# A feed-forward block in two stages: product buffers of the first, and where the operands of the second are formed

## The chip, the core and the metric

The kernel runs as one program on one core of a Trainium2 chip. The core's engines work side by side, each through its own queue of instructions in order: TensorE (PE, with PEld for its weight loads), VectorE (DVE), ScalarE (ACT), GpSimd (POOL), and SyncE (SP), which issues most of the DMAs. The metric is the device time of one execution in microseconds, as the median of several runs. Before the change it is 3231.77 us (3 runs, 3229.75 to 3237.66).

## What is computed

A two-layer encoder over 1024 tokens of width 1024. Each layer has four mixers, an output projection with a layer norm, the feed-forward block, and a gated embedding with its layer norm. The feed-forward block, with 2816 inner features, is what the change touches:

```python
gate = dwconv_centred(h @ ffn_w_gate[i], ffn_conv_w[i], ffn_conv_b[i])
f = (jax.nn.silu(gate) * (h @ ffn_w_up[i])) @ ffn_w_down[i]
h = layer_norm(ALPHA * h + f, ln2_g[i], ln2_b[i])
```

All is float32. The kernel keeps that precision by splitting each matmul operand into a high and a low part and summing three products (`p3`).

## The kernel before

The inner features are 22 tiles of 128 (`NF`). `gate_up` (L1355) goes over them one by one. Up and gate of a tile are the two rows of a 2 x 2 block product (halves of the width by halves of the tokens), and Winograd's scheme makes it in seven products of half size instead of eight. A product (`product`, L1378) is four blocks of the contraction by three terms, so 12 matmuls of 128 x 512 into one PSUM bank, from the pool `ps1` with four banks. The pool `ps2` with two tiles of two banks is not used by these products.

For each tile, `feature` (L1396) loads the up and the gate weights into two buffers (`load`, L1368, tile name wraw), forms the sum `s1` (tile s) and three differences, and splits five of them into high and low parts (`part`, L1373; ScalarE writes the high part, GpSimd or DVE the low one). The readings of PSUM are DVE additions: u and u4 (tile v) from products t2 and t1, both again from t3, c11 and c12 (tile u) from products 21 and 22, and the halves of g from t3 and t4. ScalarE reads product 11 into v1. `gated` (L1427) does the tile before: a convolution along the tokens (one ScalarE and two DVE steps), Silu on ScalarE, and the product with c11 on DVE and with c12 on GpSimd. Both halves, 256 KB each, are stored to DRAM (`fd`, L1434).

`down` (L1462) multiplies the features with the down weights. For the first 20 tiles (`PAIRED`) `down_paired` (L1511) uses the same scheme of seven products on pairs of tiles, four tiles (a chunk) at a time, so five chunks. `operands` (L1528) loads the four feature tiles (fr) and the four weight tiles (wr, wraw), forms the combinations (`comb`) of the features on DVE, with a spare tile (tg), and those of the weights on GpSimd, and splits each operand: features' low parts on GpSimd, weights' low parts on DVE (`part`, L1522). `products` (L1571) then runs 24 matmuls for each of the seven products (L1582): product 1 collects in PSUM over all chunks, products 5 to 7 are added to tiles E, the others to H, on DVE (ScalarE in the first chunk of E). The last chunk also runs `merge` (L1597). The last two tiles go a plain way (`CHUNKS`).

The program says which engine does what. The order within each engine's queue is written by a planner when the kernel is built: it takes the instructions by their place in the program as soon as it reckons their inputs and buffers to be ready. Of a pool's buffers one is taken again when its last reader is done.

Of the kernel before, what the change touches and what calls it, by code (L numbers as in the profile page):

```python
# [28 lines left out]
# columns of the packed per-layer parameters  # L29
# [4 lines left out]
# feature tiles of the input projection  # L34
# [8 lines left out]
def interleave(*flows):  # L43
    """Emits flows, each (generator, number of its steps), in step with one another."""
    live = [[g, 0, n] for g, n in flows]
    while live:
        f = min(live, key=lambda f: f[1] / f[2])
        try:
            next(f[0])
            f[1] += 1  # L50
        except StopIteration:
            live.remove(f)


def stagger(items):
    """Emits the stages of items so that each item is one stage behind the one before it."""
    items, live = iter(items), []
    while True:
        new = next(items, None)
        if new is not None:  # L60
            live.append(new)
        if not live:
            return
        for g in list(live):
            if next(g, live) is live:
                live.remove(g)
        yield
# [7 lines left out]
class Trunk:  # L75
# [70 lines left out]
    def to_x_after(self, x, H, t0, t1, ins, pair=False):  # L146
        """Transposes token tiles t0 to t1, once the products up to ins have freed the tiles that the
        result goes to."""
# [11 lines left out]
    def layer_norm(self, h, gb, eps=None, first=None):  # L160
        """The statistics; returns two functions that normalise h in place, one after the other."""
# [16 lines left out]
        def affine(c=512):  # L178
            """The first c columns, scaled already, on GpSimd, the others on VectorE."""
# [74 lines left out]
    def embed(self):  # L254
        """Normalises the input; the second half of the tokens only when the function that is returned runs."""
# [43 lines left out]
    def sin_of(self, fp, out, pre):  # L299
        """out = sin(pre) with the argument brought to [-pi, pi]."""  # L300
# [99 lines left out]
    def bruun(self, pool, zm, zp, C):  # L400
        """Residues of a polynomial of 1024 coefficients (8 blocks of 128 rows, C columns each)
        modulo the eight factors of x^2048 - 1 of degree 256; zm and zp are its residues modulo
        x^1024 - 1 and x^1024 + 1."""
# [36 lines left out]
    def conv_fft(self, l, n, pool, z, feature_major, out):  # L440
        """Circular convolution of z (token-major, 8 x 256) with filter n, and the skip term that the
        filter holds; the result is token-major [128, 8 * 256] or feature-major [128, 2, 8 * 128]."""
# [112 lines left out]
    def in_half(self, x, w, ps, hf):  # L555
        c0 = hf * 512
        if not isinstance(w, tuple):
            # the products of the high and the low parts of the weights, in separate rows
# [5 lines left out]
    def in_proj(self, l, x, tile_i):  # L564
        """One tile of 128 features, [128, 1024] in PSUM, in two steps."""
# [7 lines left out]
    def conv3(self, out, ps, cw):  # L573
        """Centred 3-tap convolution along the free dim with bias: cw columns w0, w1, w2, b."""
# [4 lines left out]
    def mixers(self, l, x, mu, late, st0):  # L579
# [9 lines left out]
        def scalars(su, ps):  # L589
            """Rotary key and dt, token-major."""  # L590
# [24 lines left out]
        def latent(pr, ti, k, rs, last, n):  # L615
            """A latent of attention with its gain, to DRAM; the sums of its squares go to rs."""
# [140 lines left out]
    def token_sums(self, sq):  # L757
        """Sums over features of the tiles sq [128 features, 512 tokens], as [128, 4] with tokens on partitions."""
# [5 lines left out]
    def squares(self, ss, g, hf, y, sq):  # L764
        """For the sums of squares of group g for 512 tokens, whose features are y, tokens on partitions:
        returns the function that finishes them on the tensor engine."""
# [6 lines left out]
    def ssd_scalars(self, l, mu, dtr):  # L773
# [5 lines left out]
        # softplus(x) = max(x, 0) + log1p(exp(-|x|)), the log by its series in e / (2 + e)  # L779
# [32 lines left out]
        # log(dt) - acs  # L812
# [6 lines left out]
    def ssd(self, l, ss, scal, xbc, zd, yd):  # L819
# [17 lines left out]
        def jv(a, c, g, n):  # L837
            """Columns (direction, head) of a group, broadcast over n."""
            return a[:, c, :].rearrange("p (d h) -> p d h", d=2)[:, :, 2 * g:2 * g + 2].unsqueeze(3).to_broadcast([128, 2, 2, n])

        def states(c, g):
            # token-major x and B, chunk states, forward scan
# [92 lines left out]
    def hl_products(self, out, terms):  # L935
        """Products of a [K, 2, 64] (hi and lo) with b, hi and lo: the sum of out[0:64] and out[64:128]."""
# [228 lines left out]
    def out_weights(self, l, g, pool):  # L1165
        """The rows of the output projection of a group, times the gains of its norm."""
# [12 lines left out]
    def out_proj(self, l, st, yd, ss, w, ahead):  # L1179
        nc, t = self.nc, self.t  # L1180
        hp = self.pool(st, f"hp{l}", 8, side=RIGHT)
        with ExitStack() as so:
# [17 lines left out]
            def scales(g):  # L1200
                # the residual branch is left unscaled: H holds the sum over ALPHA
# [73 lines left out]
    def blocks(self, todo, j):  # L1275
        """Transposes blocks of 128 tokens and 512 features, each (from, PSUM, (hi, lo)), to the
        128 tokens j of the operands."""
# [10 lines left out]
    def rest(self, l, st, H, hp, hmid, x):  # L1288
        nc, t = self.nc, self.t
        last = l == L - 1  # L1290
        fd = self.dram.tile([NF, 128, T], F32, name=f"f{l}")
# [63 lines left out]
    def gate_up(self, l, H, hp, x, fd):  # L1355
        """The inner features of the MLP, to fd. Up and gate are the two rows of a product of blocks
        A (features x halves of D) and B (halves of D x halves of the tokens), by Winograd's scheme
        of seven products."""
        nc, t, pp = self.nc, self.t, self.pp[l]
        add, sub = ALU.add, ALU.subtract  # L1360
        with ExitStack() as st:
# [16 lines left out]
            def product(w, b):  # L1378
                ps = self.one()
# [4 lines left out]
            def first(w1, w2, eng=None):  # L1384
                """The products of the first row of A and the first column of B."""
                v1, c11 = small(), fu.tile([128, 512], F32, name="u", tag="u")
# [9 lines left out]
            def feature(f, last, start=None):  # L1396
# [12 lines left out]
                w4 = part(a12, hp, "H")  # L1409
                u = small()  # L1410
                self.tt(u, product(w2, B["t2"]), v1, add)
                u4 = small()
                self.tt(u4, product(w1, B["t1"]), u, add)
# [8 lines left out]
                self.tt(g[:, 0:512], product(w22, B["t4"]), u, add)  # L1422
                c12 = fu.tile([128, 512], F32, name="u", tag="u")
                self.tt(c12, product(w4, B["22"]), u4, add)
                return f, g, c11, c12

            def gated(f, g, *cc):  # L1427
# [3 lines left out]
                for hf, c in enumerate(cc):  # L1431
                    cs = slice(hf * 512, (hf + 1) * 512)
                    self.tt(c, c, tg[:, cs], ALU.mult, nc.gpsimd if hf else nc.vector)
                    nc.sync.dma_start(fd[f][:, cs], c)  # L1434
# [8 lines left out]
            for j in range(4):  # L1443
# [3 lines left out]
                # T1 = B12 - B11, T3 = B22 - B12, T2 = B22 - T1, and B21 - T2 for T4  # L1447
# [14 lines left out]
    def down(self, l, fd, hmid, H, end, ed):  # L1462
        nc, t, pp = self.nc, self.t, self.pp[l]
        with ExitStack() as st:
# [30 lines left out]
            self.down_paired(l, fd, hmid, H, dp, ft)  # L1495
# [15 lines left out]
    def down_paired(self, l, fd, hmid, H, dp, ft):  # L1511
        """ALPHA times H plus the products of the first PAIRED inner features, by Winograd's scheme of seven
        products: A (halves of the tokens x two tiles of features) times B (the two tiles x halves of the outputs)."""
# [14 lines left out]
        def operands(ch):  # L1528
            """The operands of the seven products of two pairs of feature tiles, one after the other."""
            F, W = {}, {}  # L1530
            for k in (0, 2, 1, 3):
                f = 4 * ch + k
                F[k] = self.wp.tile([128, T], F32, name="fr", tag="whl", bufs=4)
                nc.sync.dma_start(F[k], fd[f])
# [8 lines left out]
            a11, a12, a21, a22 = ([F[2 * i + k][:, h] for i in range(2)] for h in (h0, h1) for k in range(2))  # L1543
            b11, b21, b12, b22 = ([W[2 * i + k][:, h] for i in range(2)] for h in (h0, h1) for k in range(2))
            s1 = ft.tile([128, T], F32, name="tg")
            s1 = [s1[:, h0], s1[:, h1]]
# [257 lines left out]
```

## Time and profile before

| | us |
|---|---|
| median of 3 runs | 3231.77 |
| lowest, highest run | 3229.75, 3237.66 |
| span of the profiled execution | 3236.6 |
| PE busy | 2976.9 (92%) |
| DVE busy | 2451.0 (76%) |
| GpSimd busy | 1821.3 (56%) |
| ScalarE busy | 1292.0 (40%) |
| gate and up, layer 0 (819 to 1250) | 431 |
| paired down, layer 0 (1250 to 1475) | 225 |

The span is the time from the first to the last instruction of one profiled execution. Matmuls overlap one another, so a busy PE is not a PE at its best rate. In the profile a line of the kernel can be that of a helper: L99 is every matmul of `mm`, L87 every two-operand operation of `tt`, L84 every ScalarE step. Tile names tell them apart. A timeline row gives the start, the time, the engine, the line, the operation, the written and the read tiles, the shape, the count of instructions merged, and in brackets the idle time ahead and what ended it.

### The profile page before, as it was taken

The numbers are of one execution on the slowest core, as the hardware profiler recorded it, in microseconds if no ns is written. First come the engines' busy times: TensorE is split into PE (matmuls) and PEld (weight loads), VectorE is DVE, ScalarE is ACT, GpSimd is POOL, SyncE is SP. The second block draws the span as 40 slices with busy tenths as digits, with TensorE's granted clock in tenths as the row PEclk, the third lists the DMA queues.
The fourth block names the chain that finished last, engine by engine and source line by source line (L and its number), as shares of the span: only waits on it lengthen the run. The fifth ranks groups of instructions, "written<-read, shape, count | busy, mean of one in ns | idle before, by whom it ended". The sixth has DMA issues, their size and how long they took to land.

```text
span 3236.6 us, 40462 instructions
## 1 busy us (share of the span) xinstructions
PE 2976.9 (92%) x14316; PEld 2429.1 (75%) x14316; DVE 2451.0 (76%) x3711; ACT 1292.0 (40%) x2278; POOL 1821.3 (56%) x1371
## 2 busy tenths in 40 slices
PE   6999989998999999999989998899989999989996
PEld 4887866877777777777868877778777777767685
DVE  7678776878765557999777786778786555689986
ACT  4332365743333334333343323667333333343341
POOL 5455533527656556886435454345177555578855
PEclk9999998999999999999999998999999999999998
DMA  5566523022222225313335755130222222343232
GB/s 178 156 200 204 192 75 130 16 83 85 85 79 78 78 79 198 123 47 115 126 100 172 225 192 165 53 121 25 97 85 79 79 78 78 114 163 107 74 135 92
DMA packets 140468, 368.98 MB, mean 114 GB/s; under 512 B 15139, under 2 KB 42023, under 8 KB 140009
## 3 DMA queue, kind: packets, MB, share of 16 engines
q1 hardware_dynamic: 126008, 315.72, 28.8%
q0 software_dynamic: 14256, 50.67, 5.2%
q8 instruction: 114, 1.87, 0.2%
q14 instruction: 90, 0.73, 0.1%
HBM read 278.77 MB, written 87.56 MB: 113 GB/s over the span
## 4 chain that ended last, share of the span: by engine, by line
PE 39%; DVE 21%; POOL 16%; issue 10%; DMA 10%; ACT 4%; SPq 0%; POOLq 0%; DVEq 0%; ACTq 0%
PE ps L99 18%; PE pp L99 13%; POOL w L87 5%; DMA wraw<-in_ffn_w_gate_dram 4%; POOL wraw L87 4%; DVE part L87 3%; POOL u L87 2%; DVE fr L87 2%; POOL H L87 2%; PE ps L942 2%; DVE H L90 2%; DVE s L87 1%; POOL part L87 1%; DVE H L87 1%; DMA wraw<-in_ffn_w_up_dram 1%
## 5 line engine op out<-in xcount | busy, mean ns | idle before, releaser
L99 PE MATMUL ps<-x,w 128*128 128x512 f32 x2112 | 508.2, 394 | 11.3 <-ACT v L84 6.1
L99 PEld LDWEIGHTS ps<-x,w 128*128 128x128 f32 x2112 | 400.1, 190 | 99.1 <-ACT v L84 7.0
L99 PE MATMUL pp<-x,wh 128*128 128x512 f32 x1344 | 427.9, 397 | 1.8 <-ACT wh L84 1.8
L99 PE MATMUL ps<-xq,w 128*128 128x512 f32 x1584 | 391.1, 397 | 29.7 <-DVE u L87 24.3
L1582 PE MATMUL ps<-part 128*128 128x512 f32 x1440 | 351.2, 399 | 33.8 <-DVE H L87 10.8
L99 PEld LDWEIGHTS ps<-xq,w 128*128 128x128 f32 x1584 | 292.9, 188 | 117.2 <-DVE u L87 50.7
L1582 PEld LDWEIGHTS ps<-part 128*128 128x128 f32 x1440 | 270.9, 191 | 110.5 <-DVE H L87 20.3
L99 PEld LDWEIGHTS pp<-x,wh 128*128 128x128 f32 x1344 | 254.9, 192 | 54.3 <-ACT wh L84 2.0
L87 POOL TENSOR_TENSOR w<-wraw,w 128x512 fp32r<-128x512 f32 x164 | 217.5, 1345 | 116.0 <-ACT w L84 116.0
L99 PE MATMUL pp<-x,wl 128*128 128x512 f32 x672 | 266.5, 397 | 3.8 <-POOL wl L87 3.8
L84 ACT ACTIVATE w<-wraw 128x512 fp32r<-128x512 f32 x264 | 151.8, 622 | 268.0 <-DMA wraw<-in_ffn_w_up_dram 218.6
L87 POOL TENSOR_TENSOR wl<-wraw,wh 128x1024 fp32r<-128x1024 f32 (+2 forms) x61 | 152.8, 2507 | 182.7 <-ACT wh L84 124.2
L87 POOL TENSOR_TENSOR part<-fr,part 128x512 fp32r<-128x512 f32 x120 | 192.4, 1628 | 47.2 <-ACT part L84 42.2
L87 DVE TENSOR_TENSOR s<-wraw 128x512 f32<-128x512 f32 x44 | 55.4, 1259 | 202.2 <-DMA wraw<-in_ffn_w_gate_dram 199.8
L99 PE MATMUL ps<-wo,yn 128*128 128x512 f32 x768 | 189.7, 405 | 5.4 <-DVE H L90 3.0
L1039 POOL TENSOR_TENSOR P<-P,smr 128x1024 f32<-128x1024 f32 x64 | 121.1, 1893 | 112.2 <-DVE smr L1038 103.3
L99 PEld LDWEIGHTS ps<-wo,yn 128*128 128x128 f32 x768 | 147.1, 195 | 39.4 <-DVE H L90 4.8
L90 DVE SCALAR_TENSOR_TENSOR g<-g,pp 128x1023 f32<-128x1023 f32 x88 | 126.6, 1439 | 57.7 <-ACT g L84 57.7
L87 POOL TENSOR_TENSOR u<-u,g 128x512 f32<-128x512 f32 x44 | 78.7, 1788 | 152.5 <-ACT g L84 152.3
L87 DVE TENSOR_TENSOR part<-wr,part 128x512 fp32r<-128x512 f32 x124 | 158.2, 1299 | 4.8 <-ACT part L84 4.8
L99 PE MATMUL ps<-wh,x 128*128 128x512 f32 x512 | 158.8, 391 | 0.0
L99 PEld LDWEIGHTS pp<-x,wl 128*128 128x128 f32 x672 | 128.5, 191 | 30.5 <-POOL wl L87 4.7
(381 smaller groups left out, 7038.7 us busy)
## 6 DMA issues: line engine op xcount, KB each, us to landing
c_fwd<-in_c_fwd_dram POOLq DMA_DIRECT2D x64, 512.0 KB, 5.1
wraw<-in_ffn_w_up_dram SPq DMA_DIRECT2D x50, 512.0 KB, 3.5
wraw<-in_ffn_w_gate_dram SPq DMA_DIRECT2D x44, 512.0 KB, 4.5
f<-u SPq DMA_DIRECT2D x88, 256.0 KB, 2.0
wraw<-in_w_in_dram SPq DMA_DIRECT2D x42, 512.0 KB, 4.1
fr<-f SPq DMA_DIRECT2D x40, 512.0 KB, 4.5
wr<-in_ffn_w_down_dram SPq DMA_DIRECT2D x36, 512.0 KB, 6.4
c_inv<-in_c_inv_dram POOLq DMA_DIRECT2D x32, 512.0 KB, 5.0
```

The lines of the kernel that those rows point to most:

```text
L84: self.nc.scalar.activation(out, in_, func, **kw)
L87: (eng or self.nc.vector).tensor_tensor(out, a, b, op=op)
L90: return self.nc.vector.scalar_tensor_tensor(out, a, s, b, op0=op0, op1=op1)
L99: ins = self.nc.tensor.matmul(out, a, b, start=i == 0, stop=i == n - 1)
L942: ins = self.nc.tensor.matmul(out[0:64] if j else out, v[:, 0, :] if j else v.rearrange("p i d -> p (i d)"), terms[i][1 + j], start=k == 0 ...
L1039: nc.gpsimd.tensor_tensor(P, P, sm.to_broadcast([128, T]), op=ALU.mult)
L1582: nc.tensor.matmul(ps, u, v, start=k == 0 and (p != 1 or ch == 0), stop=k == 5 and (p != 1 or ch == last))
```

## The change

`gate_up` gives four of its seven products a place in `ps2`: t2 and t1 the two halves of one tile, t4 and 22 those of a second one. For the first 20 tiles `gated` no longer stores the two halves but calls `paired`, which forms the left operands of the down scheme on DVE and stores each to a new DRAM tensor `fp`: for an even tile operands 1 and 7, for an odd one operands 2, 4, 5, 6 and 3. The tag u has six buffers instead of four, and a buffer k is added. `down_paired` loads the seven operands of a chunk as they are, through the same four buffers, and no longer forms combinations of features. Comments are taken out as well.

```diff
@@ gate_up
+        fd, fp = fd
+        kept = []
...
-            def product(w, b):
-                ps = self.one()
+            def product(w, b, ps=None):
+                ps = self.one() if ps is None else ps
...
+                lo, hi = slice(0, 512), slice(512, 1024)
+                pa = self.two()
                 u = small()
-                self.tt(u, product(w2, B["t2"]), v1, add)
+                self.tt(u, product(w2, B["t2"], pa[:, lo]), v1, add)
                 u4 = small()
-                self.tt(u4, product(w1, B["t1"]), u, add)
+                self.tt(u4, product(w1, B["t1"], pa[:, hi]), u, add)
...
-                self.tt(g[:, 0:512], product(w22, B["t4"]), u, add)
-                c12 = fu.tile([128, 512], F32, name="u", tag="u")
-                self.tt(c12, product(w4, B["22"]), u4, add)
+                pb = self.two()
+                self.tt(g[:, 0:512], product(w22, B["t4"], pb[:, lo]), u, add)
+                c12 = fu.tile([128, 512], F32, name="u", tag="u", bufs=6)
+                self.tt(c12, product(w4, B["22"], pb[:, hi]), u4, add)
                 return f, g, c11, c12
@@ gated
-                    nc.sync.dma_start(fd[f][:, cs], c)
+                    if f >= PAIRED:
+                        nc.sync.dma_start(fd[f][:, cs], c)
+                if f < PAIRED:
+                    paired(f, *cc)
+
+            def paired(f, c0, c1):
+
+                put = lambda p, v: nc.sync.dma_start(fp[f // 4, p - 1][:, f // 2 % 2], v)
+                spare = lambda: fu.tile([128, 512], F32, name="k", tag="k", bufs=1)
+                if f % 2 == 0:
+                    put(1, c0)
+                    s3 = spare()
+                    self.tt(s3, c0, c1, sub)
+                    put(7, s3)
+                    kept[:] = c0, c1
+                else:
+                    a11, s1 = kept
+                    put(2, c0)
+                    put(4, c1)
+                    self.tt(s1, s1, c1, add)
+                    put(5, s1)
+                    self.tt(a11, s1, a11, sub)
+                    put(6, a11)
+                    s4 = spare()
+                    self.tt(s4, c0, a11, sub)
+                    put(3, s4)
@@ down_paired, operands
-            F, W = {}, {}
+
+            W = {}
+
+            def left(p):
+
+                v = self.wp.tile([128, 2, 512], F32, name="fr", tag="whl", bufs=4)
+                nc.sync.dma_start(v, fp[ch, p - 1])
+                return [v[:, i] for i in range(2)]
+
+            F = {p: left(p) for p in (1, 2)}
             for k in (0, 2, 1, 3):
                 f = 4 * ch + k
-                F[k] = self.wp.tile([128, T], F32, name="fr", tag="whl", bufs=4)
-                nc.sync.dma_start(F[k], fd[f])
...
+            F.update({p: left(p) for p in (5, 7)})
...
-            yield operand(5, s1, b11)
-            comb(a21, a11, a21, sub)
-            comb(b12, b22, b12, sub, nc.gpsimd)
-            yield operand(7, a21, b12)
...
+            def operand(p, b):
+                return p, part(F[p] if p in F else left(p), nc.gpsimd), part(b, nc.vector)
...
+            yield operand(5, b11)
+            comb(b12, b22, b12, sub)
+            yield operand(7, b12)
```

## Rows read from the trace of the kernel before

**Rows 1.** Windows: busy us of PE, PEld, DVE, ACT, POOL; clock, DMA, GB/s.

```profile
core 0 of [0], span 3236.6 us
...
819.00:1250.00 431.00, 414.20 (x1769) 331.35 (x1770) 267.55 (x303) 143.44 (x212) 257.28 (x169) 1.00 0.27 90
1250.00:1475.00 225.00, 204.29 (x855) 159.85 (x853) 215.83 (x238) 89.58 (x157) 186.91 (x116) 0.98 0.32 109
2413.00:2845.00 432.00, 415.02 (x1774) 330.59 (x1775) 265.56 (x303) 143.36 (x212) 255.40 (x169) 1.00 0.27 91
2845.00:3068.00 223.00, 203.62 (x851) 159.30 (x850) 213.30 (x238) 89.60 (x157) 186.50 (x116) 0.98 0.31 108
```

**Rows 2.** Timeline of PE: start, us, line, tiles, shape, count; both stages.

```profile
830.97 2.91 PE L99 MATMUL ps<-x,w 128*128 128x512 f32 x12
...
839.21 5.66 PE L99 MATMUL ps<-xq,w 128*128 128x512 f32 x24
...
903.20 5.63 PE L99 MATMUL ps<-x,w 128*128 128x512 f32 x24
...
1229.85 5.63 PE L99 MATMUL ps<-x,w 128*128 128x512 f32 x24
...
1251.77 5.60 PE L1582 MATMUL pp<-part 128*128 128x512 f32 x24
...
1467.50 4.82 PE L1582 MATMUL ps<-part 128*128 128x512 f32 x18 [0.54 <-DVE H L87]
```

**Rows 3.** Waits of PE, 819 to 1250: us, times, longest.

```profile
PE ps L99 <- DVE u L87: 11.9, 22, 1.0
```

**Rows 4.** Timeline of all engines through one feature of gate and up.

```profile
927.33 1.51 DVE L87 TENSOR_TENSOR s<-wraw 128x512 f32<-128x512 f32 x1 [5.62 <-DMA wraw<-in_ffn_w_gate_dram]
...
935.17 0.68 DVE L87 TENSOR_TENSOR u<-ps,v 128x512 f32<-128x512 f32 x1
...
935.91 3.02 PE L99 MATMUL ps<-xq,w 128*128 128x512 f32 x12 [0.62 <-DVE u L87]
...
937.74 1.06 ACT L84 ACTIVATE g<-g 128x1024 f32<-128x1024 f32 x1 [3.61 <-DVE g L90]
...
938.88 1.81 POOL L87 TENSOR_TENSOR u<-u,g 128x512 f32<-128x512 f32 x1 [4.17 <-ACT g L84]
939.44 1.48 DVE L87 TENSOR_TENSOR v<-ps,v 128x512 f32<-128x512 f32 x2
...
940.64 2.58 POOL L87 TENSOR_TENSOR w<-wraw,w 128x512 fp32r<-128x512 f32 x2
...
941.48 2.91 PE L99 MATMUL ps<-xq,w 128*128 128x512 f32 x12
...
943.24 0.33 SPq L1370 DMA_DIRECT2D wraw<-in_ffn_w_gate_dram  x1
...
947.61 1.72 DVE L87 TENSOR_TENSOR s<-wraw 128x512 f32<-128x512 f32 x1 [5.30 <-DMA wraw<-in_ffn_w_gate_dram]
```

**Rows 5.** Windows of the down stage: in its second chunk, and a middle chunk.

```profile
1300.00:1310.00 10.00, 6.80 (x29) 5.20 (x29) 10.00 (x8) 3.28 (x7) 10.00 (x7) 0.95 0.01 2
1335.50:1375.10 39.60, 39.05 (x169) 31.22 (x168) 38.81 (x45) 15.26 (x28) 34.49 (x22) 1.00 0.31 104
```

**Rows 6.** Instructions on tile fr: least, median, greatest ns, then starts.

```profile
L87 POOL TENSOR_TENSOR part<-fr,part x120: 1274/1737/1836, 1236.0 to 3043.5; 128x512 fp32r<-128x512 f32 x120
...
L87 DVE TENSOR_TENSOR fr<-fr x40: 677/1210/1795, 1263.4 to 3021.8; 128x512 f32<-128x512 f32 x40
```

**Rows 7.** Groups of DVE by form: the three of down's combinations.

```profile
L87 DVE TENSOR_TENSOR fr<-fr 128x512 f32<-128x512 f32 x40 | 52.6, 1322 | 0.1
...
L87 DVE TENSOR_TENSOR fr<-tg,fr 128x512 f32<-128x512 f32 x20 | 23.4, 1169 | 0.0
...
L87 DVE TENSOR_TENSOR tg<-fr 128x512 f32<-128x512 f32 x20 | 22.0, 1109 | 7.0 <-DMA fr<-f 6.8
```

**Rows 8.** Window of one us in which both weight loads move.

```profile
944.00:945.00 1.00, 1.00 (x6) 0.83 (x5) 0.00 (x0) 0.00 (x0) 0.00 (x0) 1.00 0.96 385
```

More of the change, by code (lines that the diff above doesn't have):

```diff
@@ L1290, in rest @@
         last = l == L - 1
-        fd = self.dram.tile([NF, 128, T], F32, name=f"f{l}")
+        fd = self.dram.tile([NF, 128, T], F32, name=f"f{l}"), self.dram.tile([PAIRED // 4, 7, 128, 2, 512], F32, name=f"fp{l}")
         self.gate_up(l, H, hp, x, fd)
@@ L1384, in first @@
             def first(w1, w2, eng=None):
-                v1, c11 = small(), fu.tile([128, 512], F32, name="u", tag="u")
+                v1, c11 = small(), fu.tile([128, 512], F32, name="u", tag="u", bufs=6)
                 self.act(v1, product(part(w1, self.wp, "whl", eng), B["11"]))
@@ L1463, in down @@
         nc, t, pp = self.nc, self.t, self.pp[l]
+        fd, fp = fd
         with ExitStack() as st:
@@ L1493, in products @@
                                 next(filler, None)
-            self.down_paired(l, fd, hmid, H, dp, ft)
+            self.down_paired(l, fp, hmid, H, dp)
             for ch, (f0, f1) in enumerate(CHUNKS):
@@ L1509, in down, with down_paired @@
             run(filler)
-    def down_paired(self, l, fd, hmid, H, dp, ft):
+    def down_paired(self, l, fp, hmid, H, dp):
         nc, t = self.nc, self.t
@@ L1542, in operands, with comb @@
                     nc.sync.dma_start(H[tt], hmid[tt * 128:(tt + 1) * 128, :])
-            a11, a12, a21, a22 = ([F[2 * i + k][:, h] for i in range(2)] for h in (h0, h1) for k in range(2))
+            F.update({p: left(p) for p in (5, 7)})
             b11, b21, b12, b22 = ([W[2 * i + k][:, h] for i in range(2)] for h in (h0, h1) for k in range(2))
-            s1 = ft.tile([128, T], F32, name="tg")
-            s1 = [s1[:, h0], s1[:, h1]]
-            def comb(out, a, b, op, eng=None):
+            def comb(out, a, b, op):
                 for i in range(2):
-                    self.tt(out[i], a[i], b[i], op, eng)
-            def operand(p, a, b):
-                return p, part(a, nc.gpsimd), part(b, nc.vector)
-            yield operand(1, a11, b11)
-            yield operand(2, a12, b21)
-            comb(s1, a21, a22, add)
-            comb(b11, b12, b11, sub, nc.gpsimd)
-            yield operand(5, s1, b11)
-            comb(a21, a11, a21, sub)
-            comb(b12, b22, b12, sub, nc.gpsimd)
-            yield operand(7, a21, b12)
-            comb(a11, s1, a11, sub)
-            comb(b11, b22, b11, sub, nc.gpsimd)
-            yield operand(6, a11, b11)
-            comb(a12, a12, a11, sub)
-            yield operand(3, a12, b22)
-            comb(b21, b11, b21, sub, nc.gpsimd)
-            yield operand(4, a22, b21)
+                    self.tt(out[i], a[i], b[i], op, nc.gpsimd)
+            def operand(p, b):
+                return p, part(F[p] if p in F else left(p), nc.gpsimd), part(b, nc.vector)
+            yield operand(1, b11)
+            yield operand(2, b21)
+            comb(b11, b12, b11, sub)
+            yield operand(5, b11)
+            comb(b12, b22, b12, sub)
+            yield operand(7, b12)
+            comb(b11, b22, b11, sub)
+            yield operand(6, b11)
+            yield operand(3, b22)
+            comb(b21, b11, b21, sub)
+            yield operand(4, b21)
         def products(ch, p, a, b):
```

## Prediction

> **What bounds the kernel now.** I read the windows by stage first: of the two stages that the change touches, TensorE (PE) is busy 414 of 431 us in gate and up of layer 0, and 204 of 225 us in the paired down scheme, where VectorE (DVE) is busy 216 of 225 [rows 1]. Layer 1 shows the same within 3 us, so I work out one layer and double it. What PE could do at best comes from its rows without a stop: three products of 12 matmuls take 839.21 - 830.97 = 8.24 us, 2.747 us each, 0.229 us a matmul [rows 2]. A feature of gate and up has seven products, 19.23 us; the period in the trace is (1229.85 - 903.20) / 16 = 20.42 us [rows 2], so each feature loses 1.2 us, 24 over the some 20 features that lose it. The paired down scheme has 5 x 168 = 840 matmuls, 192 us, and takes 1467.50 + 4.82 - 1251.77 = 220.5 us [rows 2], a loss of 28 us.
>
> The table of waits puts the loss in gate and up on PE waiting 22 times for DVE u, the reading of a PSUM bank [rows 3]: in one feature PE stops at 935.91, just as DVE ends the reading that began at 935.17 [rows 4]. This is where I part from that table. Why does DVE read so late? Follow one feature backward through its own rows [rows 4]: s (927.33) opens DVE's chain of splits, readings and convolution, behind which ScalarE's Silu runs 937.74 to 938.80, GpSimd multiplies u by g (938.88 to 940.69), then splits two weight tiles (to 943.22); that frees the raw weight tile, SP issues the gate load at 943.24, and DVE, idle for 5.30 us on that DMA, forms the next s at 947.61. The ring is closed, 927.33 to 947.61 is 20.3 us, and no step in it waits for PE. So PE's stops are an effect: the ring of DVE, ScalarE, GpSimd and one load paces the features, PE needs only 19.23.
>
> In down, DVE is 39 of 39.6 us busy in a middle chunk, GpSimd 34.5 [rows 5]; there DVE is the bound, with GpSimd near it.
>
> **The change, part by part.** (1) *Both PSUM pools.* Four of seven products move from the pool of four banks to halves of two-bank tiles, of which there are two. In an unchanged ring this buys only a lead: the two-bank tile of t4 and 22 comes round every second tile, so PE's next t4 (941.48) could start when c12 of the feature before is read (935.17 + 0.68 = 935.85) [rows 4], 5.6 us earlier, once per layer. I take -5 us a layer; bounds 0 (the start of down waits for its loads anyway) and -6. Matmuls, readings and their sizes stay as they are.
>
> (2) *Forming the operands in gate and up.* It does so for 20 of 22 features. An even one stores c0 and s3: 1 DVE operation more, the same 2 stores. An odd one has 3 DVE operations in a chain (s1, a11, s4) and 5 stores instead of 2. c1 of the even feature is kept and not stored. So 40 operations and 30 stores of 256 KB a layer are put behind the GpSimd product, which ends at 940.69. What hides them on DVE: the 5.30 us idle ahead of s; at 0.68 us (alone) to 1.8 (beside GpSimd) [rows 6] (the least and the greatest of such an operation) three take 2.0 to 5.4 us, so DVE itself has room, or just. What doesn't hide: three things of the ring lie in the same stretch.
> First, SP: its queue is in order, and the stores are ready before the gate load is freed, so I expect all of an odd feature's stores ahead of that load. With 1.25 us an operation (between the ends, near the means in [rows 7]) s4 ends at 940.69 + 3.75 = 944.44, its store is issued by 944.8, and the gate load that went out at 943.24 goes at 944.8, +1.55 us. Queued behind it is all of the next feature's prologue: s, both weight differences, their splits.
> Second, DMA: up and gate run at 385 GB/s with the engines 0.96 busy [rows 8], so 256 KB ahead of them costs 0.68 us; three stores 2.0 us, part of it inside the same 1.55.
> Third, GpSimd's two splits: the same kind of split takes 1.27 us alone and 1.84 beside DVE [rows 6], up to 0.57 more for each; this too overlaps the SP delay. The Trainium skill (SBUF — State Buffer, Who interferes with whom) calls the pair of ports that VectorE and GpSimd share an exclusive lock, which a VectorE operation with two SBUF inputs takes; by that rule an odd feature's three operations of 0.68 us would add up to 2.0 us to GpSimd's splits, so +2.0 in place of the +1.55 below and +25 a layer in place of +20; the trace's 0.57 for each agrees in kind.
> I take +1.55 for an odd and +0.45 for an even feature (its second store moves 1.25 us later, no bytes are added, one split is stretched), 1.0 on average, x 20 = +20 us a layer. Bounds: 0.5 (only the bytes) to 1.65 (bytes and SP one after the other), +10 to +33. A gain from this part is excluded unless the order changes; that is a rival. The next feature has the delay in full because the ring has no slack. Sum of gate and up: 20 - 5 = +15 us a layer, +5 to +28.
>
> (3) *Down without its combinations.* 80 DVE operations leave, 52.6 + 22.0 + 23.4 = 98.0 us in both layers [rows 7], 49 us of DVE's 216 in each [rows 1]. What is late next: PE with 192, and GpSimd, 187 now [rows 1], of which each of 116 operations is stretched up to 0.57 us by DVE; fewer DVE operations shorten it. The feature loads go from 4 to 7 of 512 KB a chunk, +1.5 MB in some 40 us, on engines that are 0.31 busy in a middle chunk [rows 5]; but they go through four buffers that are now freed operand by operand, where before a chunk's four stayed until its last operands. That tells on the first two chunks: in 1300 to 1310 PE is busy 6.8 of 10 us, DVE and GpSimd 10 of 10, DMA 0.01 [rows 5]: the loads are over, and both engines still catch up on their splits. I take 18 of the 28 us that PE loses; bounds 10 (GpSimd becomes the bound) and 24 (only fills and the last merges are left). Added to SP's queue: 15 loads a layer, 0.33 us each, in front of nothing that PE waits for while the four buffers hold.
>
> **Sum.** +15 - 18 = -3 us a layer, -6 in all. The profiled execution's span is 3236.6 us [rows 1], 4.8 above the median of 3231.77 and inside the runs shown (3229.75 to 3237.66); the sum is made on its rows and carried over as a difference: 3231.8 - 6 = 3226 us. This case alone spans (5 - 24) x 2 = -38 to (28 - 10) x 2 = +36: 3194 to 3268.
>
> **Rivals.** *The cover holds:* the operations fall into DVE's idle 5.30 us and the gate load is issued ahead of the stores. For it: the idle time is there in every feature. Against: GpSimd's product, which makes the stores ready, ends 2.5 us before the load is freed. Gate and up -5, down -18: -46, 3186 us.
> *PSUM was the bound:* with eight banks PE no longer stops, and the features take PE's 19.23 us. It needs the ring to run faster than its rows, so another order of DVE's work. For it: the table of waits; against it: the ring without PE. Gate and up -24, down -18: -84, 3148 us. The Trainium skill (Perfetto Trace Analysis, Optimization Strategy) says that a gap repeating on the engine that should be saturated can mean too little PSUM for the next tile; by that rule this rival is the forecast, and the ring in the trace speaks against it.
> *The ring stretches twice as far (slower):* DVE puts three readings of PSUM (u4, g, u; 0.68 each) between the chained operations, so the odd gate load leaves 2.0 us later still, and bytes follow: odd +3, even +1, 2.0 x 20 = +40 - 5; down gains 12. (35 - 12) x 2 = +46, 3278 us. It decides from +1.15 us a feature on: there 23 - 5 equals the 18 that down gives. For it: the readings begin at 939.44 [rows 4], on the spot.
> *Down is not relieved (slower):* GpSimd's splits and combinations, 34.5 us of a chunk [rows 5], take the place of DVE; down gains 4. (15 - 4) x 2 = +22, 3254 us. Against it: GpSimd's stretch comes from the very operations that leave.
>
> **How the numbers follow.** Forecast 0.50, cover holds 0.20, PSUM the bound 0.07, ring twice as far 0.15, down not relieved 0.08. About 0.3%, 9.7 us, can be told from no change: faster is below 3222, slower above 3241.5. The forecast's own case lies 0.21 / 0.18 / 0.11 on faster, same, slower; with the rivals 0.48, 0.18, 0.34. The range leaves out the PSUM case, the lowest of the second and the upper half of the stretched ring: 3172 to 3278.
>
> **What would show it.** Right: the feature period in gate and up goes from 20.4 to about 21.4 us, odd ones longer than even ones; SP's row of the gate load stands behind the stores; PE still stops, now in front of t4; DVE in down falls from 216 to some 165 us and a middle chunk from 40 to 39. Wrong: a period at or under 20.4 (cover or PSUM rival), at 22.4 (ring twice as far), or down still above 215 us (GpSimd). The weakest number is the order on SP and DVE, which the rows of before cannot show.

## The result, and the profile after

The kernel after takes 3195.99 us (median of 4 runs, 3189.56 to 3203.33) beside 3233.77 for the kernel before on the same chip: a ratio of 0.9883, interval 0.9867 to 0.9899, 38 us less. The forecast was 3226 us. The sign and the range held; the size did not: some 30 of the 38 us were not in the sum, and the nearest case is the rival "the cover holds" (3186).

The profiled execution's span is 3192.7 us, 43.9 below the one before. In both stages, windows of after (the columns of [rows 1]; each window starts at the stage's first product, as PE's timeline shows it; the last one is a middle chunk of down):

```profile
813.80:1239.30 425.50, 410.50 (x1764) 330.91 (x1765) 305.44 (x342) 143.18 (x212) 241.63 (x170) 1.00 0.33 108
1239.30:1444.30 205.00, 197.49 (x854) 160.45 (x854) 167.81 (x195) 88.68 (x154) 173.45 (x113) 0.99 0.48 159
1320.00:1359.00 39.00, 39.00 (x174) 32.30 (x173) 33.44 (x40) 15.37 (x28) 34.58 (x24) 1.00 0.45 149
```

Gate and up took 431.9 us before in the same measure and 425.5 now, down 220.6 and 205.0; layer 1 shows 432.2 to 425.7 and 219.4 to 204.9. So gate and up, forecast 15 us a layer longer, are 6.4 shorter, and down is 15 shorter where 18 were forecast. That makes 43 in two layers; the stages that the change does not touch moved by -6 and +5 us, which leaves the 44 of the spans. A middle chunk is at PE's own pace, 39.0 of 39.0 us, and DVE in down fell from 216 to 168 [rows 1, 5].

PE's waits in gate and up from 825 to 1235, the answer to [rows 3] (us, times, longest), are scattered over small causes:

```profile
PE pp L99 <- DVE v L87: 5.4, 5, 1.6
PE ps L99 <- ACT v L84: 2.4, 5, 0.9
PE pp L99 <- DVE g L87: 2.3, 3, 1.3
PE ps L99 <- DVE w L87: 1.1, 1, 1.1
```

One feature of after in the timeline of all engines, the answer to [rows 4] (an odd tile, so five stores). Here u*g is the product of Silu's result with c11 on DVE and with c12 on GpSimd:

```profile
927.55 0.82 DVE L87 TENSOR_TENSOR s<-wraw 128x512 f32<-128x512 f32 x1 [4.29 <-DMA wraw<-in_ffn_w_gate_dram]
...
937.96 0.69 DVE L87 TENSOR_TENSOR u<-u,g 128x512 f32<-128x512 f32 x1 [1.19 <-ACT g L84]
...
938.53 1.31 POOL L87 TENSOR_TENSOR w<-wraw,w 128x512 fp32r<-128x512 f32 x1 [5.41 <-ACT w L84]
938.57 0.68 DVE L87 TENSOR_TENSOR u<-pp,v 128x512 f32<-128x512 f32 x1
...
939.79 1.31 POOL L87 TENSOR_TENSOR u<-u,g 128x512 f32<-128x512 f32 x1
939.86 0.33 SPq L1372 DMA_DIRECT2D wraw<-in_ffn_w_up_dram  x1
...
941.05 1.31 POOL L87 TENSOR_TENSOR w<-wraw,w 128x512 fp32r<-128x512 f32 x1
941.12 2.13 SPq L1446 DMA_DIRECT2D fp<-u  x2
...
943.36 0.37 SPq L1372 DMA_DIRECT2D wraw<-in_ffn_w_gate_dram  x1
...
943.78 0.44 SPq L1446 DMA_DIRECT2D fp<-u  x1
944.23 2.54 POOL L87 TENSOR_TENSOR w<-wraw,w 128x512 fp32r<-128x512 f32 x2 [1.87 <-ACT w L84]
944.39 0.32 SPq L1446 DMA_DIRECT2D fp<-k  x1
...
947.57 0.69 DVE L87 TENSOR_TENSOR s<-wraw 128x512 f32<-128x512 f32 x1 [3.21 <-DMA wraw<-in_ffn_w_gate_dram]
```

Rows of the kernel before that stand between those of [rows 4]:

```profile
938.83 0.69 DVE L87 TENSOR_TENSOR u<-u,g 128x512 f32<-128x512 f32 x1 [1.19 <-ACT g L84]
...
941.98 0.33 SPq L1370 DMA_DIRECT2D wraw<-in_ffn_w_up_dram  x1
...
946.25 2.54 POOL L87 TENSOR_TENSOR w<-wraw,w 128x512 fp32r<-128x512 f32 x2 [3.03 <-ACT w L84]
```

The ring is still there, but GpSimd's order in it is another. Before, it did u*g and then the low parts of w22 and w4; now w22, u*g, w4. The first of the two ends frees a weight buffer, so the up load leaves 3.5 us ahead of the gate load (939.86, 943.36), where it left 1.26 us ahead before (941.98, 943.24). SP issues the gate load ahead of the last two of the five stores, not behind them all. s, at 947.57, takes 0.69 us and not 1.72. Nothing in the diff asks for this order; the planner wrote it. By GpSimd's rows, u*g stands first in 18 of 20 tiles of layer 0 before and in 4 after; of the other 16, five have it last, behind both splits.

### The profile page after: what moved, and what is told of

Same layout as the page of the kernel before. It is cut to its first block, busy times and chain, and to the rows that moved or that the text cites. A ratio compares the mean times of both kernels' runs of the same rounds, so it can differ in the third digit from the quotient of the medians.

```text
span 3192.7 us, 40546 instructions
## 1 busy us (share of the span) xinstructions
PE 2946.4 (92%) x14316; PEld 2420.9 (76%) x14316; DVE 2440.4 (76%) x3711; ACT 1291.6 (40%) x2278; POOL 1771.2 (55%) x1371
## 4 chain that ended last, share of the span: by engine, by line
PE 48%; DVE 22%; POOL 9%; DMA 8%; issue 8%; ACT 5%; SPq 0%; DVEq 0%; POOLq 0%; ACTq 0%
PE ps L99 17%; PE pp L99 15%; PE ps L1613 7%; DMA wraw<-in_ffn_w_gate_dram 4%; POOL H L87 2%; DVE g L90 2%; DVE u L87 2%; PE ps L942 2%; DVE w L87 2%; POOL w L87 2%; DVE H L90 2%; PE ps L1054 1%; DVE v L87 1%; ACT w L84 1%; POOL wraw L87 1%
## 5 line engine op out<-in xcount | busy, mean ns | idle before, releaser
L1613 PE MATMUL ps<-part 128*128 128x512 f32 x1440 | 341.4, 393 | 14.7 <-DVE H L87 6.1
L87 POOL TENSOR_TENSOR w<-wraw,w 128x512 fp32r<-128x512 f32 x164 | 232.7, 1431 | 206.0 <-ACT w L84 205.8
L99 PE MATMUL ps<-x,w 128*128 128x512 f32 x1056 | 261.6, 395 | 10.8 <-ACT v L84 10.8
L99 PE MATMUL pp<-x,w 128*128 128x512 f32 x1056 | 258.3, 394 | 14.1 <-DVE v L87 9.7
L99 PE MATMUL pp<-xq,w 128*128 128x512 f32 x1056 | 264.4, 392 | 5.8 <-DVE x L87 4.5
L99 PEld LDWEIGHTS pp<-x,w 128*128 128x128 f32 x1056 | 196.9, 188 | 63.7 <-DVE v L87 13.8
L87 POOL TENSOR_TENSOR part<-fr,part 128x512 fp32r<-128x512 f32 x140 | 220.5, 1602 | 43.7 <-ACT part L84 43.4
L99 PEld LDWEIGHTS ps<-x,w 128*128 128x128 f32 x1056 | 199.0, 190 | 59.9 <-ACT v L84 18.0
L99 PEld LDWEIGHTS pp<-xq,w 128*128 128x128 f32 x1056 | 198.0, 188 | 51.2 <-ACT w L84 5.1
```

The source lines that it names most:

```text
L87: (eng or self.nc.vector).tensor_tensor(out, a, b, op=op)
L99: ins = self.nc.tensor.matmul(out, a, b, start=i == 0, stop=i == n - 1)
L1613: nc.tensor.matmul(ps, u, v, start=k == 0 and (p != 1 or ch == 0), stop=k == 5 and (p != 1 or ch == last))
```

## The experiments

The period is the mean from gate load to gate load of tiles 6 to 20 in both layers (20.45 us before, 19.55 after); stages are measured as above, as a mean of both layers (gate and up 432.0 before, 425.6 after; down 220.0 and 205.0).

**Each part alone.** First, only the four products' tiles (the run keeps the stores and the down stage of before).

```diff
-                self.tt(u, product(w2, B["t2"]), v1, add)
+                pa = self.two()
+                self.tt(u, product(w2, B["t2"], pa[:, lo]), v1, add)
... the same for t1, t4 and 22
```

> The kernel before with one part of the change: products t2, t1, t4 and 22 go to the halves of the two-bank tiles. No operand is formed in gate and up, down is as before. Theory of the prediction (the ring paces, banks buy a lead once): the feature period stays at 20.4 us, gate and up is 0 to 6 us shorter a layer, down stays at 220 us, so 3234 - 10 = 3224 us. Rival (the planner lays out a new order of VectorE's work once banks are free, and the ring closes faster): period 19.2 to 19.8 us, gate and up 13 to 25 us shorter a layer, 3184 to 3208 us.

Measured: 3229.99 us, ratio 0.9983 (0.9972 to 0.9994). Gate and up 425.8, 6 less; down 223.9, 4 more, since it starts earlier and waits for its loads. Period 19.9. The total is as forecast, 5 us less. u*g is first in 9 of 20 tiles, so this run has the banks and half of another order. The two can be told apart in its own gate loads: in layer 0 the periods with u*g first (tiles 8 to 15) are 20.6 to 21.0 us, those behind them with w22 first (tiles 17 to 21) 18.1 to 19.2; in the kernel before, tiles 17 to 21 take 20.4 to 20.7.

Then after with all seven products in the pool of four banks:

```diff
-                self.tt(u, product(w2, B["t2"], pa[:, lo]), v1, add)
+                self.tt(u, product(w2, B["t2"]), v1, add)
... the same for t1, t4 and 22
```

> The kernel after without the PSUM part: all seven products stay in the pool of four banks, the operands are formed and stored in gate and up and loaded ready by down. Theory of the prediction: the added operations, stores and waits lengthen the feature period by about 1.0 us, to 21.4, +20 us a layer, and down falls by 15 us a layer (measured in the kernel after): 3234 + 40 - 30 = 3244 us. Rival (the added work is covered by VectorE's idle time ahead of s): period 20.4, 3234 - 30 = 3204 us.

Measured: 3241.82 us, ratio 1.0024 (1.0012 to 1.0036). Gate and up 451.8, 20 more; period 21.4, odd tiles 23.5, even ones 19.2; down 202.1, 18 less. The prediction's means came out. So the terms were met one by one, -6, +20 and -18, and their sum was not: with both parts, gate and up takes 20 us a layer less than -6 + 20 gives. The timeline of an odd tile here:

```profile
941.07 0.69 DVE L87 TENSOR_TENSOR u<-u,g 128x512 f32<-128x512 f32 x1 [1.19 <-ACT g L84]
941.11 1.81 POOL L87 TENSOR_TENSOR u<-u,g 128x512 f32<-128x512 f32 x1 [4.18 <-ACT g L84]
...
942.88 3.02 POOL L87 TENSOR_TENSOR w<-wraw,w 128x512 fp32r<-128x512 f32 x2
...
945.18 0.38 SPq L1372 DMA_DIRECT2D wraw<-in_ffn_w_up_dram  x1
...
946.37 0.68 DVE L87 TENSOR_TENSOR v<-ps,v 128x512 f32<-128x512 f32 x1
...
947.67 0.32 SPq L1444 DMA_DIRECT2D fp<-k  x1
...
948.08 0.39 SPq L1372 DMA_DIRECT2D wraw<-in_ffn_w_gate_dram  x1
...
952.57 0.69 DVE L87 TENSOR_TENSOR s<-wraw 128x512 f32<-128x512 f32 x1 [3.12 <-DMA wraw<-in_ffn_w_gate_dram]
```

GpSimd's splits end at 945.90, the gate load leaves at 948.08, behind the store of s4: the predicted queue on SP. u*g is first in 18 of 20 tiles, as before.

**The order or the banks.** Two theories of the missing 20 us: with eight banks the ring has room (theory "room"), or the order in the ring is what pays. First, after with u*g first:

```diff
+                with self.tc.issue_after(late[0].ins) if late else ExitStack():
-                w22 = part(a22, hp, "H")
+                    w22 = part(a22, hp, "H")
...  late[0] is the GpSimd u*g of two tiles before
```

> The kernel after, with one edge of issue order on GpSimd: the subtraction that splits a feature's w22 is issued behind the product u*g of two features before (the order of the kernel before), where after has w22, u*g, w4. The theory 'a new order': what paid is that the first of a feature's two weight buffers comes free ahead of u*g, so that the next up load leaves 3.5 us ahead of the gate load and not 1.3; taken back, a feature goes from 19.55 us to 19.9 (the period of the products' banks alone, where most u*g went first) or above, gate and up 7 us a layer longer or more, the whole 3210 or above. The theory 'room': with eight banks TensorE's own pace (19.23 us a feature) sets the period and the ring of DVE, ScalarE, GpSimd, SP and gate load has room; then a feature stays within 0.1 us of 19.55 and the whole lies at 3191 to 3201.

Measured: 3253.53 us, ratio 1.0056 (1.0041 to 1.0071): slower than before, with all of the change in it. Gate and up 450.8, period 21.1. With u*g first, eight banks are no shorter than four were (451.8).

```profile
946.38 0.69 DVE L87 TENSOR_TENSOR u<-u,g 128x512 f32<-128x512 f32 x1
946.99 0.68 DVE L87 TENSOR_TENSOR u<-pp,v 128x512 f32<-128x512 f32 x1
...
947.81 1.30 POOL L87 TENSOR_TENSOR u<-u,g 128x512 f32<-128x512 f32 x1 [5.49 <-ACT w L84]
949.06 3.02 POOL L87 TENSOR_TENSOR w<-wraw,w 128x512 fp32r<-128x512 f32 x2
...
951.36 0.38 SPq L1372 DMA_DIRECT2D wraw<-in_ffn_w_up_dram  x1
...
953.38 0.32 SPq L1447 DMA_DIRECT2D fp<-k  x1
...
953.79 0.39 SPq L1372 DMA_DIRECT2D wraw<-in_ffn_w_gate_dram  x1
```

The gate load is behind the last store again. But the run is more than a swap. DVE reads c12 (u<-pp,v) behind its own u*g, and GpSimd's u*g, which needs c12, starts 1.43 us behind DVE's (946.38, 947.81); with the four banks of the run before it started 0.04 behind (941.07, 941.11). The orders of PE, DVE and ScalarE differ from after's as well. So the 25 us a layer above after are not the price of the swap alone, and this run does not give the worth of the banks at an order that is otherwise the same.

Then the other way round, the operands on four banks with the order of after: the second half of `gated` (u*g on GpSimd, DVE's forming and the stores behind it) is traced one tile later, right behind w22's split, with an edge to it.

```diff
                 w22 = part(a22, hp, "H")
+                if late:
+                    late.pop()(self.low.ins)
...
+                def second(ins=None):
+                    with self.tc.issue_after(ins) if ins is not None else ExitStack():
+                        self.tt(cc[1], cc[1], tg[:, 512:1024], ALU.mult, nc.gpsimd)
...
+                late.append(second)
```

> The operands alone on four banks (as in e2), with the order of after on GpSimd: w22's subtraction, then u*g, then w4's. The theory 'a new order': the order can be had without the banks, so a feature falls from 21.4 us to 20.4 or less, gate and up 20 us a layer shorter, the whole at 3195 to 3222. The theory 'room': the banks themselves are needed, a feature stays at 21.3 to 21.5 us and the whole at 3237 to 3246.

Measured: 3200.57 us, ratio 0.9893 (0.9876 to 0.9909). Gate and up 431.5, 20 less than with u*g first; period 20.2 and 20.5. Four banks come within 5 us of the kernel after. PE and ScalarE keep their order; DVE's changes with GpSimd's, as the forming moves.

```profile
940.64 0.69 DVE L87 TENSOR_TENSOR u<-u,g 128x512 f32<-128x512 f32 x1 [1.19 <-ACT g L84]
941.21 1.30 POOL L87 TENSOR_TENSOR w<-wraw,w 128x512 fp32r<-128x512 f32 x1 [4.70 <-ACT w L84]
...
942.54 0.33 SPq L1372 DMA_DIRECT2D wraw<-in_ffn_w_up_dram  x1
...
946.02 0.37 SPq L1372 DMA_DIRECT2D wraw<-in_ffn_w_gate_dram  x1
...
947.05 0.32 SPq L1452 DMA_DIRECT2D fp<-k  x1
```

The same edge in the kernel before, without banks or operands:

> The kernel before, four banks and whole features stored, with one edge of issue order on GpSimd: u*g is issued behind w22's subtraction (the order that after has in most features), so w22, u*g, w4 in every feature. The theory 'a new order, whatever the banks and the stores': with the operands on four banks the same edge gave 20 us a layer; here a feature falls from 20.4 us to 19.4 or 19.6 and the whole to 3198 to 3212. The rival 'the order pays only where seven stores a pair stand ahead of the gate load': moving these stores off SP gave 12 of the 20 us, so 8 us a layer are left, the whole at 3214 to 3224. The rival 'the order pays only with the operands': within 4 us of before.

Measured: 3205.16 us, ratio 0.9901 (0.9887 to 0.9916), 30 us less than before. Gate and up 417.2, the shortest of all the kernels; period 19.6 and 19.7; down 218.6. A tile here, and PE's waits from 825 to 1240:

```profile
939.98 0.69 DVE L87 TENSOR_TENSOR u<-u,g 128x512 f32<-128x512 f32 x1 [1.19 <-ACT g L84]
940.55 1.31 POOL L87 TENSOR_TENSOR w<-wraw,w 128x512 fp32r<-128x512 f32 x1 [4.69 <-ACT w L84]
...
941.81 1.31 POOL L87 TENSOR_TENSOR u<-u,g 128x512 f32<-128x512 f32 x1
941.89 0.33 SPq L1371 DMA_DIRECT2D wraw<-in_ffn_w_up_dram  x1
...
944.41 0.33 SPq L1371 DMA_DIRECT2D wraw<-in_ffn_w_gate_dram  x1
...
948.22 1.15 DVE L87 TENSOR_TENSOR s<-wraw 128x512 f32<-128x512 f32 x1 [4.75 <-DMA wraw<-in_ffn_w_gate_dram]
...
959.37 0.69 DVE L87 TENSOR_TENSOR u<-u,g 128x512 f32<-128x512 f32 x1 [1.19 <-ACT g L84]
```

```profile
PE ps L99 <- DVE v L87: 3.0, 1, 3.0
PE ps L99 <- DVE u L87: 1.9, 4, 0.8
```

Three sections of the ring, here and in [rows 4]: DVE's u*g to the gate load's issue, 944.41 - 939.98 = 4.43 us (4.41 before); issue to s, 3.81 (4.37); s to the next u*g, 959.37 - 948.22 = 11.15. The up load leaves 1.91 us behind DVE's u*g, not 3.15, and no longer side by side with the gate load. PE waited 11.9 us for DVE u in [rows 3]; 1.9 are left, with the same four banks.

This is the cleanest of the pairs. By the tiles that they read and write, PE, ScalarE and DVE (335 operations) go through gate and up in the same order as before, in both layers; only GpSimd's order differs, and with it SP's, where the second store now stands behind the up load. SP holds nothing back here: in both kernels the gate load leaves within 0.05 us of the end of the split that frees its buffer (943.22 and 943.24, 944.38 and 944.41).

Last, the edge in after itself, so that no tile has u*g first:

> The kernel after with the same edge: after itself has w22, u*g, w4 on GpSimd in 12 of the features of a layer and u*g first in 3 of the last six; with the edge no feature has u*g first. If the order sets the period, the last features fall from 20.0 to 21.4 us to about 19.6, gate and up 3 to 6 us a layer shorter, the whole at 3183 to 3191, faster than both kernels. If these features are long for another reason, the whole stays within 3 us of after's 3196.

Measured: 3193.52 us, ratio 0.9870 (0.9853 to 0.9886), not to be told from after. The mean period fell to 19.3 and 19.5, the down stage to 203.3, gate and up to 424.1: 1.5 us a layer, not 3 to 6, and less than the 4 us by which its two layers differ.

**What the forming costs.** The operands on four banks, the stores issued by ScalarE; PE and GpSimd keep their order.

```diff
-                put = lambda p, v: nc.sync.dma_start(
+                put = lambda p, v: nc.scalar.dma_start(
```

> The operands alone on four banks (as in e2), with the seven stores of a pair issued by ScalarE instead of SP; TensorE's and GpSimd's order stays the same. The predicted step 'the gate load stands behind the stores on SP': in e2's odd features the gate load left 2.2 us behind the end of the subtraction that freed its buffer, behind the store of s4; without that an odd feature falls from 23.5 us to 21.3, the mean from 21.4 to 20.3, gate and up 23 us a layer shorter than e2's, the whole about 3196. The rival 'it is the forming itself': VectorE's 1.6 us of an odd feature or the transfers' bytes delay the ring; then the mean stays at 21.0 or above and the whole at 3230 or above, more if ScalarE's queue holds its evictions behind a store.

Measured: 3222.77 us, ratio 0.9961 (0.9946 to 0.9976). Gate and up 440.0, 12 less, half of what was expected. Odd tiles fell from 23.5 to 21.1 us, as expected, but even ones rose from 19.2 to 20.3: part of what an odd tile lost had been made up in the even one.

```profile
940.99 3.29 ACTq L1444 DMA_DIRECT2D fp<-u  x3
...
944.33 0.63 ACT L84 ACTIVATE w<-wraw 128x512 fp32r<-128x512 f32 x1 [3.57 <-DMA fp<-u]
...
945.11 1.31 POOL L87 TENSOR_TENSOR w<-wraw,w 128x512 fp32r<-128x512 f32 x1 [1.73 <-ACT w L84]
```

The run has a cost of its own: ScalarE's high part of w4 stands behind three stores that wait for DVE, and GpSimd idles 1.73 us for it ahead of the split that frees the gate load's buffer. So I read SP's queue as at least 12 of the 20 us; what it is without that cost was not run.

The operands on four banks, without DVE's forming:

```diff
-                    self.tt(s3, c0, c1, sub)
-                    put(7, s3)
+                    put(7, c1)
... likewise s1, a11 and s4
```

> The operands alone on four banks (as in e2) without VectorE's forming: the four additions and subtractions of a pair are left out and unformed values are stored in their place (the result is another), with as many stores and bytes. If the forming (with the stores that wait for it) is what stretched the ring, a feature falls from 21.4 us to 20.4 to 20.6 and the whole to 3200 to 3210; if the bytes or the number of stores are what stretched it, a feature stays at 21.2 or above and the whole at 3236 or above.

Measured: 3213.35 us, ratio 0.9940 (0.9925 to 0.9955); gate and up 437.8, 14 less, period 20.6 and 20.8. It lies between both expectations, near the first: the forming, with the stores that wait for it, is 14 of the 20, and 6 stay with the stores themselves. This 14 and the 12 or more of SP's queue overlap, as the store that holds the gate load waits for s4.

The same edit in after:

> The kernel after without VectorE's forming of operands in gate and up: the four additions and subtractions of a pair are left out and unformed values are stored in their place (the result is another), with as many stores and bytes; the loads in down stay. The theory 'room': the forming is covered there, a feature stays within 0.1 us of 19.55, gate and up within 3 us a layer, the whole at 3190 to 3200. The rival 'the forming still costs its time in the ring': 0.5 us a feature less, 19.0 to 19.2 (TensorE's pace allows 19.23), gate and up 7 us a layer shorter, the whole at 3182 or below.

Measured: 3204.96 us, ratio 0.9913 (0.9896 to 0.9930): longer than after with less work, and neither theory said so. Gate and up 431.2, period 20.2 and 20.0, tiles alternating between 24 and 17 us. GpSimd's order is another again, u*g first in 8 of 20 tiles. Less work did not shorten it; I read the new order as the cause, but no run fixed the order here.

And after with its stores on ScalarE, the diff of the first run of this group:

> The kernel after with the seven stores of a pair issued by ScalarE instead of SP. The theory 'room': the gate load's place on SP no longer counts, a feature stays within 0.15 us of 19.55 and the whole at 3190 to 3202. The rival 'the ring still sets the pace': the gate load, which left 1.0 us behind the end of GpSimd's second split, leaves at once, a feature falls to 19.25 to 19.3 (TensorE's pace) and the whole to 3182 to 3186; if ScalarE's evictions queue behind stores, it is longer than after.

Measured: 3205.62 us, ratio 0.9922 (0.9907 to 0.9936). Gate and up 430.0, period 19.9 and 19.8, u*g first in 8 of 20. Longer than after, as the expectation allowed if ScalarE's work queues behind stores, but the order has changed too, so the run doesn't tell the theories apart.

**Room in the ring.** s done twice (one more DVE addition a tile), in before and in after:

```diff
                 self.tt(s1, a21, a22, add)
+                self.tt(s1, a21, a22, add)
```

> The kernel before, with VectorE's addition s, which waits for the gate load, done twice: 0.68 us more in the ring of each feature. The predicted step 'the ring sets the pace, with no room': a feature goes from 20.42 us to 21.1, gate and up 15 us a layer longer, the whole about 3264. The rival 'TensorE's stops set the pace through the banks, and the ring has room': a feature stays within 0.15 us of 20.42, the whole within 7 us of 3234.

Measured: 3246.72 us, ratio 1.0045 (1.0030 to 1.0061). Gate and up 438.7, 6.7 more; from tile 7 on, where GpSimd's order is that of before, the mean period went from 20.4 to 20.75 us, by half of the added 0.68. So the ring has little room, but some: not none, as I had put it.

> The kernel after, with VectorE's addition s, which waits for the gate load, done twice: 0.69 us more in the ring of each feature. The theory 'room': the ring has that much room, a feature stays at 19.55 to 19.7 us, the whole at 3194 to 3203. The rival 'the ring still sets the pace': a feature takes 20.2 us, gate and up 15 us a layer more, the whole about 3226.

Measured: 3241.49 us, ratio 1.0025 (1.0013 to 1.0037). Gate and up 445.4, 20 more, period 20.9: beyond the rival too. The planner's order had changed, u*g first in 8 of 20 tiles, alternating with the other order. As 0.69 us of work can't account for 1.3 us a tile, this run shows the order's weight and leaves after's room open.

## Why the prediction was right and wrong

**The ring sets the pace, PE's stops are an effect.** Right. The edge in before touches neither PE nor a bank, leaves the order of PE, DVE and ScalarE as it was, and took PE's waits for DVE u from 11.9 to 1.9 us and 15 us off a layer. "No slack" was too strong (half of 0.68 us was absorbed).

**In an unchanged ring the banks only buy a lead, -5.** The number was met (-6 in gate and up, 5 us in all), but by luck: the ring did not stay unchanged. Half of that run's tiles took w22 first and were shorter; those with u*g first were longer than before, not equal. With w22 first, the banks bring 431.5 to 425.6 (after) or 424.1 (with the edge), 6 to 7 us a layer, where the layers of the first and the last of these three differ by 4 to 5. No run has eight banks with every other order as before. The Trainium skill (Perfetto Trace Analysis, Optimization Strategy) says that a repeated gap on the engine to be saturated can mean too little PSUM; the runs agree only in part, since the gap closed with the same four banks.

**Forming, +20.** Met at the order of before: +20. At the order of after it is 431.5 - 417.2 = +14. The split over odd and even tiles was wrong: +3.1 and -1.2, where I had +1.55 and +0.45. An odd tile lost what the rival "the ring stretches twice as far" gave it (+3), and in part for its reason: one reading of PSUM (946.37 with four banks) stands among the chained operations, not three. That the mean came out is partly luck, since an even tile makes up part of what the odd one lost.

**Down, -18.** Right in kind, 15 of 18: DVE at 168 us (forecast 165), a middle chunk at 39.0 (39). In the runs on four banks it was 18.

**The sum.** This is the step that failed: "A gain from this part is excluded unless the order changes; that is a rival." I priced both parts on the order that the rows showed, and kept the new order for a rival with 0.07, tied to PSUM as the bound. The order did change, on GpSimd rather than on DVE, and by itself it is worth 15 us a layer. From kernel to kernel, gate and up went by -15 (order, 432.0 to 417.2), +14 (forming at that order, to 431.5) and -6 (banks, to after's 425.6), in all -6.4. These steps join before to after, so that they add up is no test of them; each is the price of one part on the order of the kernel ahead of it. With down's -15 it makes -43 in two layers. The rival "the cover holds" gave nearly the measured time for another reason: on four banks the forming is not free at either order.

**Why the order pays.** Moving w22 ahead of u*g frees a buffer one GpSimd operation sooner, and the up load gets a start of 2.5 to 3.5 us on the gate load in place of 1.26. In the tile shown of before with the edge, the gate load to s is 0.56 us shorter, and s to u*g another 0.56 (from 947.61 to 959.32 before, 11.71). With the seven stores, the gate load also goes ahead of s4's. GpSimd's splits of the up weights move forward by the same step: in before they begin at 946.25 and s runs beside them in 1.72 us; in after they are over when s begins, and it takes 0.69. The Trainium skill (SBUF — State Buffer, Who interferes with whom) says of the two engines that "Issue order, not op shape, decides who blocks". The rows of before agree: the splits began first and kept 2.54 us for two, as in after, and s was stretched. That the order pays is shown by before and its edge, where nothing but GpSimd's and SP's order differs, and borne out by the four-bank pair with operands, where DVE's differs too, and by after and its reverse, where every engine's does. How much of it each of these three steps carries is argued from the rows alone.

**Why eight banks bring that order.** The rows suggest it. Before, DVE reads c12 at 935.17 [rows 4], ahead of its own u*g; in after it reads it at 938.57, behind it. GpSimd's u*g needs c12 and can't start before 939.25, while w22's split starts at 938.53. In tiles 2 to 20 of both layers, every kernel here with eight banks reads c12 between DVE's u*g and GpSimd's; none with four banks does so in any tile. So the banks change the order by way of one reading on DVE. That the planner chose for this reason wasn't tested, and in 4 of 20 tiles of after it chose otherwise.

**Still open.** How much room the ring of after has. Nor is it shown why gate and up with eight banks take 424 us at a period of 19.4 where before with the edge takes 417 at 19.65; the first five periods, 99.7 us there and 91.2 here in layer 0, put the difference in the first tiles. The 417 and the 202 of down on four banks have no kernel in common: the 202 needs the operands, and with these the same order takes 431.5.

## What to carry to other kernels

Where a planner writes the order, an edit changes two things, the work and the order, and a sum over the rows of before prices only the first: ask which in-order queue lies in the ring that sets the pace, and what one swap in it would be worth. Test that swap alone, before a change that brings it by the way: one edge of issue order in the old kernel gave 30 of the 38 us that this change gave. When parts measured alone add up to another number than both together, compare the order of each engine before you look for a cost.

## What the runs showed of the hardware

I had bounded GpSimd's split beside DVE by 1.84 us, the greatest in [rows 6]. With s done twice in after such GpSimd operations went beyond that, next to two convolution steps of DVE that took 3.53 us (2.59 in after):

```profile
956.40 3.53 DVE L90 SCALAR_TENSOR_TENSOR g<-g,pp 128x1023 f32<-128x1023 f32 x2
956.55 2.29 POOL L87 TENSOR_TENSOR wraw<-s,wraw 128x512 f32<-128x512 f32 x1 [3.09 <-DVE wraw L87]
...
958.80 2.29 POOL L87 TENSOR_TENSOR w<-s,w 128x512 fp32r<-128x512 f32 x1
```

Alone such a GpSimd operation takes 1.3 us in after. In these rows both engines take longer than without the overlap, so which operations meet is part of the price of an order.
